# A two-layer encoder on one core: the memory heads' queries as a turned product, with 1/rms in their softmax

## The chip, the core and the metric

The kernel runs on one core of one Trainium2 chip. Its time is the device time of one execution in microseconds (us). A program measures it several times, and the kernel before has a median of 1112.88 us over three runs (1111.99 to 1113.64). TensorE (PE in the profile) multiplies and transposes, VectorE (DVE), ScalarE (ACT) and GpSimd (POOL) do the rest, and SyncE (SP) starts the transfers.

## What is computed

512 tokens of width 1024 pass through two layers. Each layer adds a token mixer with memory heads and then a gated feed-forward block (inner width 2816). The first layer's mixer is a banded attention with a sink, the second's a global one with normed queries and keys. The part that matters here is the memory heads: four heads of width 64 whose queries come from the tokens and whose keys and values come from a memory of 256 tokens.

```python
h = rms_norm(x, g_mix_pre[i])
proj = h @ w_in[i]
qm = proj[..., Q_W + 2 * KV_W:].reshape(B, S, N_MEM_HEADS, HEAD_DIM)
...
mkv = mem_n @ w_mem_kv[i]
km = mkv[..., :QM_W].reshape(B, N_MEM, N_MEM_HEADS, HEAD_DIM)
vm = mkv[..., QM_W:].reshape(B, N_MEM, N_MEM_HEADS, HEAD_DIM)
s = jnp.einsum('bshd,bmhd->bhsm', qm, km) * ATTN_SCALE
p = jax.nn.softmax(s, axis=-1)
o = jnp.einsum('bhsm,bmhd->bshd', p, vm)
```

The token heads are 12, in three groups of four with one key head each. Their outputs and the memory heads' stand side by side and go through `w_o`.

## The kernel before

Each product of fp32 numbers is made of three matmuls. A number is split into a high part (a copy rounded to the short form that TensorE takes, L286 on ScalarE or L284 on GpSimd) and a low part (the number less its high part, L290 on VectorE or L288 on GpSimd). The three products are high by high, high by low and low by high (L276, L277, L278). Weights come from memory whole, as `raw`, and are split into `whi` and `wlo`. The normed tokens are kept turned (feature on partition, token on column) as `hT`, high and low, in eight blocks of 128 features. The factor 1/rms of a token is not in `hT`; it is a column `rs` with one value for each token, and `rq` is that column times -1/8, so that queries carry the scale of the scores with a negative sign.

*Queries.* `q_pieces` (L520 to L567) makes them in chunks of four heads: c = 0, 1, 2 for the token heads, c = 3 for the memory heads. For each of four tiles of 128 tokens, eight steps of three matmuls hold a piece of `hT` as weights and let 256 columns of `whi` or `wlo` move past it, into a bank `acc` of the accumulator memory. The result, tokens on partitions, is copied out with the scale `rq` or `rs` (L538, L540, ScalarE). The token heads then get their rotary products (L440 to L443 in the first layer). The queries are split (L286, L290), four transposes (L558) of the pair [high, low] bring each head to the form feature by token, and ScalarE copies the result to `qT` (L559).

*Keys.* `keys` (L420 to L430) transposes a tile of keys twice: once as [high, low], copied by ScalarE (L426), and once as [low, high], through the bank `pv`, copied by VectorE (L430). The arrays are `ka` and `kb` for the token heads, and `kma` and `kmb` for the memory heads. A score is then two matmuls that each use all 128 rows: [q high, q low] by [k high, k low] and by [k low, k high].

*Memory heads.* `score_mem` (L600 to L620) takes two tiles of queries at a time. The scores go to a bank of the ring `s`; since the queries are negative, VectorE takes the minimum as `nm` (L614), and ScalarE computes the exponential of -1 times the score plus `nm` (L617), with the sum as `den`. Once a head's sums are there, VectorE takes the reciprocal `rd` (L630) and GpSimd multiplies p by it (L633). `turn` transposes p (L643) and splits it into `th` and `tl`; `value` multiplies it by the values (L657, L658), and a copy and an addition (L665, L666) put the result into `tok`.

*What sets the order.* Only TensorE's order is written by hand. Every piece of work is handed to `put(x, f)` with a position x in units of one head, from the table `PACE`, and the pieces run in the order of x. The tiles of queries c = 3 stood at positions from 7 + `qoff[2]` on, one `qstep` apart, among the scores, turns and values of the token heads. A scheduler orders the other engines' work. The banks limit it: two `acc`, three `s` (two once the output projection has taken the third), one `pv`, two `t`.

Of the kernel before, what the change touches and what calls it, by code (L numbers as in the profile page):

```python
# [185 lines left out]
class Trunk:  # L186
# [232 lines left out]
    def keys(self, k2, ka, kb, t, n):  # L419

        nc = self.nc
        tp = self.ps.tile([P, 4, P], F32, tag="t", name="tp", bufs=2)
        for h in range(n):
            nc.tensor.transpose(tp[:, h].bitcast(F32R), k2[:, h, :P], self.identr)
        c = slice(t * P, (t + 1) * P)
        nc.scalar.activation(ka[:, :, c], tp[:, :n], AF.Copy)  # L426
        tp = self.tagged("pv", "tp").rearrange("p (h n) -> p h n", n=P)
        for h in range(n):
            nc.tensor.transpose(tp[:, h].bitcast(F32R), k2[:, h, HD:], self.identr)
        nc.vector.tensor_copy(kb[:, :, c], tp[:, :n])  # L430


    def halves(self, x):
# [82 lines left out]
    def q_pieces(self, l, c, qTs, put, x0, lead):  # L516
# [6 lines left out]
        def prod(t, st, u):  # L523
            self.ready(t)
            if c not in qTs:
                qTs[c] = self.core.tile([P, 4, S], F32R, tag="qT", name="qT", bufs=2)
            if u == 0:
                st["ps"] = self.ps.tile([P, 512], F32, tag="acc", name="ps", bufs=2)
            ps = st["ps"]
            for k in (2 * u, 2 * u + 1):  # L530
                cs = slice((k % 4) * 256, (k % 4) * 256 + 256)
                self.mm3(ps[:, :256], self.hslice(0, k, t * P, t * P + P), self.hslice(1, k, t * P, t * P + P),
                         w[k // 4][0][:, cs], w[k // 4][1][:, cs], k == 0, k == KD - 1)
            if u == 3:
                qx = self.core.tile([P, 4, HD], F32, tag="qx", name="qx", bufs=3)
                q = ps[:, :256].rearrange("p (h d) -> p h d", d=HD)
                if l == 1 and c < 3:
                    nc.scalar.activation(qx, q, AF.Copy, scale=self.rs[:, t:t + 1])  # L538
                else:
                    nc.scalar.activation(qx, q, AF.Copy, scale=self.rq[:, t:t + 1])  # L540
                st["qx"], st["r"] = qx, None
                if c < 3:
                    st["r"] = self.rope(l, qx, t, 4, 0)

        def parts(st):
            qx, r = st["qx"], st["r"]
# [4 lines left out]

        def stage(t, st):
            if c:
                tp = self.tagged("s" if c == 3 and t > 1 else "acc", "tp").rearrange("p (h n) -> p h n", n=P)
            else:
                tp = self.ps.tile([P, 4, P], F32, tag="t", name="tp", bufs=2)
            for h in range(4):
# [7 lines left out]
                        lambda t=t, st=st: stage(t, st), lambda st=st: parts(st)))  # L565
        return out


    def score(self, hd, i):
        nc = self.nc  # L570
# [29 lines left out]
    def score_mem(self, hd, i):  # L600
# [9 lines left out]
        for z in range(2):  # L610
            qi = hd["q"]()[:, (i + z) * P:(i + z + 1) * P]
            nc.tensor.matmul(s[:, z], qi, hd["ka"](), start=True, stop=False)
            nc.tensor.matmul(s[:, z], qi, hd["kb"](), start=False, stop=True)
        nc.vector.tensor_reduce(nm[:, i:i + 2], s, axis=AX.X, op=OP.min)  # L614
        for z in range(2):
            p = self.core.tile([P, self.pbufs[0]], F32, tag="p", name="p", bufs=self.pbufs[1])
            nc.scalar.activation(p[:, :NMEM], s[:, z], AF.Exp, bias=nm[:, i + z:i + z + 1], scale=-1.0,  # L617
                                 accum_out=den[:, i + z:i + z + 1])
            hd["p"].append(p)
        if i == 2:  # L620
# [62 lines left out]
    def mixer(self, l, mkp, late, tokp):  # L683
# [68 lines left out]
        xm.append(xm[2] + pc["mdur"])  # L752
        xw = [xm[0] - pc["m0lead"], xm[1] - pc["m0lead"] + 0.01, xm[2] - pc["mlead"], xm[3] - pc["mlead"] + 0.01]
        self.mem_pieces(l, mk, put, xm, [pc["m0dur"], pc["m0dur"], pc["mdur"], pc["mdur"]], pc["mlag"], xw)
        for c in range(1, 4):
            x0 = 4 * c - 5 + pc["qoff"][c - 1]
            lay(self.q_pieces(l, c, qT, put, x0, pc["qlead"]), x0, pc["qstep"], pc["qlag"], lambda t, c=c: 4 * c + (t / 4 if c < 3 else t // 2 / 2 * pc["hstep"]))
        heads()
        xs = [max(2 * z + 1 + pc["lag"] + pc["vlag"] + 3 * pc["jstep"], 7 + 4 * pc["qstep"] + pc["qoff"][2] + pc["hoff"]) + 0.01
              for z in range(6)]  # L760
# [608 lines left out]
```

## Time and profile before

| | |
|---|---|
| median of three runs | 1112.88 us (1111.99 to 1113.64) |
| the profiled execution's own time | 1110.48 us |
| its span from first to last instruction | 1108.7 us |
| granted clock of TensorE, mean over the span | 0.999 |
| busy: TensorE, VectorE, ScalarE, GpSimd | 98%, 76%, 59%, 18% of the span |

The profile gives one execution. The mean time of an instruction is from its start to its end; on TensorE neighbours overlap, so the sum of busy times there is larger than the time that passes, and the step from one start to the next is what a matmul costs. A number in brackets at the end of a row, as in `[1.20 <-DVE kmb L430]`, is the time in which the engine had nothing to run, and the work that ended it. The memory heads' queries are computed between about 80 and 140 us in the first layer and 640 and 700 us in the second.

### The profile page before, as it was taken

Reading aid. Unit: us, or ns where it says so; the run is one execution under the profiler, and the core shown is the slowest. Engines: PE = TensorE matmul, PEld = TensorE weight load, DVE = VectorE, ACT = ScalarE, POOL = GpSimd, SP = SyncE. Lnnn points to the kernel's source line nnn. Section 1 sums busy time; section 2 is a strip of 40 time slices with the busy share of each in tenths; the row PEclk is TensorE's granted clock in tenths of the full one; section 3 lists DMA queues with packets and bytes.
Section 4 is the critical chain, followed back from the end, with each engine's and each line's share of the span. In section 5 each row is a group of like instructions: output and inputs, shape, how many; then the busy total and the mean of one; then the engine's idle time right before and its main releaser. Section 6 shows DMA issues by size and latency. Waiting matters only on the chain.

```text
span 1108.7 us, 19514 instructions
## 1 busy us (share of the span) xinstructions
PE 1089.4 (98%) x7438; PEld 1000.2 (90%) x7438; DVE 840.7 (76%) x1433; ACT 658.5 (59%) x1356; POOL 196.2 (18%) x342
## 2 busy tenths in 40 slices
PE   8999999999999999999999999999999999999997
PEld 7989978999889989998898888879999899899986
DVE  7789875999558767875788988758995478669854
ACT  6679975765445534563567888756664366346631
POOL 5683331102000000000443542212000000000001
PEclk9999999999999999999999999999999999999999
DMA  8621017343833472325543221145136123322243
GB/s 319 224 98 40 25 33 266 115 153 127 308 116 108 152 248 76 115 92 189 186 143 114 77 77 38 39 172 171 59 112 213 56 95 115 134 72 98 82 168 114
DMA packets 40558, 142.44 MB, mean 128 GB/s; under 512 B 4624, under 2 KB 5008, under 8 KB 40336
## 3 DMA queue, kind: packets, MB, share of 16 engines
q1 hardware_dynamic: 40176, 140.66, 36.8%
q8 instruction: 58, 0.95, 0.4%
q10 hardware_dynamic: 288, 0.53, 0.2%
q14 instruction: 36, 0.29, 0.1%
HBM read 122.30 MB, written 18.87 MB: 127 GB/s over the span
## 4 chain that ended last, share of the span: by engine, by line
PE 88%; DVE 5%; ACT 2%; POOL 2%; issue 1%; DMA 1%; DVEq 0%; POOLq 0%; SPq 0%; ACTq 0%
PE ps L277 14%; PE ps L276 14%; PE ps L278 14%; PE ps L1042 12%; PE ps L1041 12%; PE ps L1040 12%; PE tp L643 3%; PE o L658 2%; PE o L657 2%; PE s L582 1%; PE s L583 1%; DVE tl L290 1%; POOL r L310 1%; DVE tok L666 1%; ACT junk L314 1%
## 5 line engine op out<-in xcount | busy, mean ns | idle before, releaser
L286 ACT ACTIVATE whi<-raw 128x1024 fp32r<-128x1024 f32 (+3 forms) x205 | 168.5, 839 | 176.9 <-PE ps L1042 73.5
L290 DVE TENSOR_TENSOR wlo<-raw,whi 128x1024 fp32r<-128x1024 f32 (+3 forms) x202 | 190.9, 960 | 73.5 <-ACT whi L286 71.5
L1041 PE MATMUL ps<-sf,wlo 128*128 128x256 f32 x640 | 179.8, 281 | 0.0
L1040 PE MATMUL ps<-sf,whi 128*128 128x256 f32 x640 | 179.7, 281 | 0.0
L1042 PE MATMUL ps<-sf,whi 128*128 128x256 f32 x640 | 179.7, 281 | 0.0
L276 PE MATMUL ps<-whi,f 128*128 128x512 f32 (+1 forms) x360 | 138.7, 385 | 0.0
L277 PE MATMUL ps<-wlo,f 128*128 128x512 f32 (+1 forms) x360 | 138.5, 385 | 0.0
L278 PE MATMUL ps<-whi,f 128*128 128x512 f32 (+1 forms) x360 | 138.4, 385 | 0.0
L1042 PE MATMUL ps<-a,whi 128*128 128x256 f32 x480 | 134.4, 280 | 0.0
L1040 PE MATMUL ps<-a,whi 128*128 128x256 f32 x480 | 134.4, 280 | 0.0
L1041 PE MATMUL ps<-a,wlo 128*128 128x256 f32 x480 | 133.8, 279 | 0.0
L1041 PEld LDWEIGHTS ps<-sf,wlo 128*128 128x128 f32 x640 | 121.4, 190 | 0.5
L1040 PEld LDWEIGHTS ps<-sf,whi 128*128 128x128 f32 x640 | 121.1, 189 | 0.5
L1042 PEld LDWEIGHTS ps<-sf,whi 128*128 128x128 f32 x640 | 121.4, 190 | 0.0
L319 POOL TENSOR_SCALAR e<-sso 128x1 f32<-128x1 f32 x8 | 3.4, 420 | 563.9 <-ACT junk L314 563.7
L276 PE MATMUL ps<-whi,hT 128*128 128x256 f32 (+1 forms) x312 | 95.2, 305 | 0.0
L633 POOL TENSOR_SCALAR p<-p,rd 128x256 f32<-128x256 f32 (+2 forms) x128 | 76.5, 615 | 101.0 <-DVE rd L630 43.2
L277 PE MATMUL ps<-wlo,hT 128*128 128x256 f32 (+1 forms) x312 | 91.1, 292 | 2.9 <-DVE wlo L290 2.9
L278 PE MATMUL ps<-whi,hT 128*128 128x256 f32 (+1 forms) x312 | 90.9, 291 | 0.0
L1041 PEld LDWEIGHTS ps<-a,wlo 128*128 128x128 f32 x480 | 90.5, 188 | 0.2
L1040 PEld LDWEIGHTS ps<-a,whi 128*128 128x128 f32 x480 | 90.4, 188 | 0.2
L1042 PEld LDWEIGHTS ps<-a,whi 128*128 128x128 f32 x480 | 90.1, 188 | 0.0
(209 smaller groups left out, 2703.6 us busy)
## 6 DMA issues: line engine op xcount, KB each, us to landing
raw<-in_wgu_dram SPq DMA_DIRECT2D x48, 512.0 KB, 4.3
raw<-in_wd_dram SPq DMA_DIRECT2D x44, 512.0 KB, 4.4
rb<-in_wgu_dram SPq DMA_DIRECT2D x40, 512.0 KB, 3.6
raw<-in_wo_dram SPq DMA_DIRECT2D x17, 512.0 KB, 3.7
raw<-in_wq_dram SPq DMA_DIRECT2D x16, 512.0 KB, 5.3
xt<-x SPq DMA_DIRECT2D x12, 512.0 KB, 4.7
raw<-in_wm_dram SPq DMA_DIRECT2D x8, 512.0 KB, 4.0
x<-y SPq DMA_DIRECT2D x8, 512.0 KB, 3.0
```

The source lines that it names most:

```text
L276: mm(out, lh, rh, start=first, stop=False)
L277: mm(out, lh, rl, start=False, stop=False)
L278: mm(out, ll, rh, start=False, stop=last)
L286: a = nc.scalar.activation(hi, src, AF.Copy)
L290: b = nc.vector.tensor_sub(lo, src, hi.bitcast(F32))
L633: self.pooled = nc.gpsimd.tensor_scalar(hd["p"][z][:, :n], hd["p"][z][:, :n], rd[:, z:z + 1], 1.0, op0=OP.mult, op1=OP.mult)
L643: nc.tensor.transpose(tp[:, z], hd["p"][i][:, jj * P:(jj + 1) * P], self.ident)
L657: nc.tensor.matmul(o[:, c0:c1], hd["v"](j), th, start=(j == 0), stop=False, skip_group_check=True)
L658: nc.tensor.matmul(o[:, c0:c1], hd["v"](j), tl, start=False, stop=last, skip_group_check=True)
L1040: mm(out, wh[:, s], rh, start=start and k == 0, stop=False, skip_group_check=True)
L1041: mm(out, wl[:, s], rh, start=False, stop=False, skip_group_check=True)
L1042: mm(out, wh[:, s], rl, start=False, stop=k == 3, skip_group_check=True)
```

## The change

Three things are altered.

1. The memory heads' queries leave `q_pieces`. A new function `memory_queries` makes them turned from the start: for each of two halves z (two heads, 128 columns of the weight), the columns of `whi` and `wlo` are held as weights and all 512 tokens of `hT` move past them, eight steps of three matmuls into one bank `acc`. Feature is on partition and token on column, so no transpose follows. ScalarE copies the two heads' high parts to `qT`, 64 rows by 512 columns each, and VectorE writes the two low parts, 64 by 512 each, into the other 64 rows. For the second head of a half the high part stands in the lower rows of `qT` and the low part in the upper, so its halves are the other way round; since both orders of the keys are used in the sum, the score is the same.
2. 1/rms of a token varies along the columns there, so the queries stay without it. The scores of a pair of tiles have tokens on partitions, and the factor comes in there: VectorE takes the maximum `mx`, multiplies it by `rq` to give `nm`, and the exponential takes its scale from the column `rp` = -`rq`, which GpSimd makes once a layer.
3. In `keys`, the memory keys' second copy (four heads) goes to ScalarE; the token keys' stays with VectorE.

The eight steps of each half stand a quarter of `qstep` apart, from the same first position as before, so that both halves together take the span that the four tiles took.

```diff
@@ keys
-        nc.vector.tensor_copy(kb[:, :, c], tp[:, :n])
+        if n == NMH:
+            nc.scalar.activation(kb[:, :, c], tp[:, :n], AF.Copy)
+        else:
+            nc.vector.tensor_copy(kb[:, :, c], tp[:, :n])
@@ q_pieces: stage
-                tp = self.tagged("s" if c == 3 and t > 1 else "acc", "tp").rearrange("p (h n) -> p h n", n=P)
+                tp = self.tagged("acc", "tp").rearrange("p (h n) -> p h n", n=P)
@@ new
+    def memory_queries(self, l, qTs, put, x0, lead, step):
+
+        nc = self.nc
+        w, ps = {}, {}
+        for z in range(2):
+            self.unit(self.a["wq"][l, 3, z], self.side(l, "qw", 6 + z), put=put, x=x0 - lead + z * lead / 3, dst=w,
+                      key=z, pair=("wq", l, 3, z))
+
+        def prod(z, k):
+            if k == 0:
+                ps[z] = self.tagged("acc")
+            c = slice((k % 4) * 256 + P * z, (k % 4) * 256 + P * z + P)
+            wh, wl = [x[:, c] for x in w[k // 4]]
+            self.mm3(ps[z], wh, wl, self.hslice(0, k, 0, S), self.hslice(1, k, 0, S), k == 0, k == KD - 1)
+            if k < KD - 1:
+                return
+            if z == 0:
+                qTs[3] = self.core.tile([P, 4, S], F32R, tag="qT", name="qT", bufs=2)
+                self.rp = self.small.tile([P, NT], F32, tag="rp", name="rp", bufs=2)
+                nc.gpsimd.tensor_scalar(self.rp, self.rq, -1.0, 1.0, op0=OP.mult, op1=OP.mult)
+            rows = (slice(0, HD), slice(HD, P))
+            q = [qTs[3][:, 2 * z + h] for h in range(2)]
+            for h in range(2):
+                nc.scalar.activation(q[h][rows[h]], ps[z][rows[h]], AF.Copy)
+            for h in range(2):
+                nc.vector.tensor_sub(q[h][rows[1 - h]], ps[z][rows[h]], q[h][rows[h]].bitcast(F32))
+
+        for z in range(2):
+            for k in range(KD):
+                put(x0 + (2 * z + k / 4) * step, lambda z=z, k=k: prod(z, k))
@@ score_mem
-        nc.vector.tensor_reduce(nm[:, i:i + 2], s, axis=AX.X, op=OP.min)
+        mx = self.small.tile([P, 2], F32, tag="mx", name="mx", bufs=3)
+        nc.vector.tensor_reduce(mx, s, axis=AX.X, op=OP.max)
+        nc.vector.tensor_mul(nm[:, i:i + 2], mx, self.rq[:, i:i + 2])
...
-            nc.scalar.activation(p[:, :NMEM], s[:, z], AF.Exp, bias=nm[:, i + z:i + z + 1], scale=-1.0,
+            nc.scalar.activation(p[:, :NMEM], s[:, z], AF.Exp, bias=nm[:, i + z:i + z + 1],
+                                 scale=self.rp[:, i + z:i + z + 1],
                                  accum_out=den[:, i + z:i + z + 1])
@@ the mixer's list of pieces
-        for c in range(1, 4):
+        for c in range(1, 3):
             x0 = 4 * c - 5 + pc["qoff"][c - 1]
-            lay(self.q_pieces(l, c, qT, put, x0, pc["qlead"]), x0, pc["qstep"], pc["qlag"], lambda t, c=c: 4 * c + (t / 4 if c < 3 else t // 2 / 2 * pc["hstep"]))
+            lay(self.q_pieces(l, c, qT, put, x0, pc["qlead"]), x0, pc["qstep"], pc["qlag"], lambda t, c=c: 4 * c + t / 4)
+        self.memory_queries(l, qT, put, 7 + pc["qoff"][2], pc["qlead"], pc["qstep"])
```

Three places show what it does to the order. The first is TensorE in the first layer, where the third tile's product, or now the second half's, begins. Here `ps` is the bank of the queries, `tp` a transpose, `p` the softmax of a token head, `th` and `tl` its split transpose, and `o` a head's output. A row names the output, then the moving operand and the weights. Before:

```order
L276 MATMUL ps_1917<-whi_1582,hT_115 128x256
L277 MATMUL ps_1917<-wlo_1583,hT_115 128x256
L278 MATMUL ps_1917<-whi_1582,hT_117 128x256
L643 MATMUL tp_1924<-cst_87,p_1718 128x128
L643 MATMUL tp_1924<-cst_87,p_1742 128x128
L643 MATMUL tp_1924<-cst_87,p_1763 128x128
L558 MATMUL tp_1932<-identr_91,q2_1834 128x128 x4
L657 MATMUL o_1938<-th_1869,vs_246 128x256
L658 MATMUL o_1938<-tl_1870,vs_246 128x256
```

and after:

```order
L276 MATMUL ps_1891<-hT_115,whi_1582 128x512
L277 MATMUL ps_1891<-hT_117,whi_1582 128x512
L278 MATMUL ps_1891<-hT_115,wlo_1583 128x512
L678 MATMUL tp_1895<-cst_87,p_1714 128x128
L678 MATMUL tp_1895<-cst_87,p_1735 128x128
L678 MATMUL tp_1895<-cst_87,p_1753 128x128
L692 MATMUL o_1903<-th_1841,vs_246 128x256
L693 MATMUL o_1903<-tl_1842,vs_246 128x256
```

Each group of three narrow products with `hT` as weights (two of them stand there before, one is shown) has become one of three wide products with the weight matrix as weights, and the group L558 behind the turn is gone.

The second place is VectorE at the end of the second half, where `tok` is written for a token head, `nm` is the maximum of a tile and `q2` a tile of queries before its transpose. Before:

```order
L666 TENSOR_TENSOR tok_888<-o_2051,tmp_2130 64x512
L629 TENSOR_TENSOR den_2023<-den_2023,es_2114 128x4
L588 ISA p_2154,nm_2149<-s_2151,mask_210,nsink_89 128x256
L588 ISA nm_2149 128x1
L630 RECIPROCAL rd_2113<-den_2023 128x4
L290 TENSOR_TENSOR tl_2146<-tp_2141,th_2145 128x384
L290 TENSOR_TENSOR tl_2168<-tp_2163,th_2167 128x384
L588 ISA p_2183,nm_2149<-s_2180,mask_210,nsink_89 128x384
L588 ISA nm_2149 128x1
L290 TENSOR_TENSOR q2_2186<-qx_2139,q2_2186 128x4x64
```

and after:

```order
L701 TENSOR_TENSOR tok_888<-o_1992,tmp_2062 64x512
L664 TENSOR_TENSOR den_1974<-den_1974,es_2046 128x4
L620 ISA p_2085,nm_2080<-s_2082,mask_210,nsink_89 128x256
L620 ISA nm_2080 128x1
L665 RECIPROCAL rd_2045<-den_1974 128x4
L595 TENSOR_TENSOR qT_1868<-ps_1891,qT_1868 64x512 x2
L290 TENSOR_TENSOR tl_2077<-tp_2072,th_2076 128x384
L290 TENSOR_TENSOR tl_2099<-tp_2094,th_2098 128x384
L620 ISA p_2108,nm_2080<-s_2105,mask_210,nsink_89 128x384
L620 ISA nm_2080 128x1
```

The two subtractions of the second half stand ahead of the two `tl`; the last tile's split, which stood behind them, is gone.

The third place is VectorE in the first layer while the memory keys are made. There `rt` and `qx` belong to the rotary products of a tile of queries, and `den`, `es` and `rd` to the first token head. Before:

```order
L430 CAST kmb_816<-tp_929 128x4x128
L588 ISA p_938,nm_879<-s_935,mask_210,nsink_89 128x256
L588 ISA nm_879 128x1
L440 TENSOR_TENSOR rt_958<-qx_956,cst_87 128x64
L442 TENSOR_TENSOR qx_956<-qx_956,cst_87 128x4x16
L430 CAST kmb_816<-tp_968 128x4x128
L629 TENSOR_TENSOR den_880<-den_880,es_942 128x4
L443 TENSOR_TENSOR qx_956<-qx_956,rt_958 128x4x16
L630 RECIPROCAL rd_941<-den_880 128x4
```

and after:

```order
L620 ISA p_938,nm_879<-s_935,mask_210,nsink_89 128x256
L620 ISA nm_879 128x1
L664 TENSOR_TENSOR den_880<-den_880,es_942 128x4
L665 RECIPROCAL rd_941<-den_880 128x4
L620 ISA p_979,nm_974<-s_976,mask_210,nsink_89 128x256
L620 ISA nm_974 128x1
L443 TENSOR_TENSOR rt_958<-qx_956,cst_87 128x64
L445 TENSOR_TENSOR qx_956<-qx_956,cst_87 128x4x16
L446 TENSOR_TENSOR qx_956<-qx_956,rt_958 128x4x16
```

Both copies L430 are gone from VectorE, `den` and `rd` have moved up to right behind the last maximum, and the three rotary products stand behind the next head's first maximum.

More of the change, by code (lines that the diff above doesn't have):

```diff
@@ L536, in prod @@
                 q = ps[:, :256].rearrange("p (h d) -> p h d", d=HD)
-                if l == 1 and c < 3:
+                if l:
                     nc.scalar.activation(qx, q, AF.Copy, scale=self.rs[:, t:t + 1])
@@ L540, in prod @@
                     nc.scalar.activation(qx, q, AF.Copy, scale=self.rq[:, t:t + 1])
-                st["qx"], st["r"] = qx, None
-                if c < 3:
-                    st["r"] = self.rope(l, qx, t, 4, 0)
+                st["qx"], st["r"] = qx, self.rope(l, qx, t, 4, 0)
         def parts(st):
```

## The prediction, made before the changed kernel ran

> **What bounds the kernel now.** I read the totals first, then the chain that ended last, then the windows of the stage that the change touches, and last the timeline around each wait in it.
>
> ```profile
> PE 1089.4 (98%) x7438; PEld 1000.2 (90%) x7438; DVE 840.7 (76%) x1433; ACT 658.5 (59%) x1356; POOL 196.2 (18%) x342
> PE 88%; DVE 5%; ACT 2%; POOL 2%; issue 1%; DMA 1%; DVEq 0%; POOLq 0%; SPq 0%; ACTq 0%
> ```
>
> TensorE is busy 98% of the span and holds 88% of the chain: a TensorE instruction that goes is worth its step, as long as nothing else is late just behind it. That has to be asked of each stretch, so the windows come next (window: length, then busy us of PE, PEld, DVE, ACT, POOL).
>
> ```profile
> 80.00:110.00 30.00, 29.46 (x233) 28.36 (x234) 26.94 (x87) 27.13 (x79) 11.42 (x19) 1.00 0.12 36
> 110.00:126.00 16.00, 16.00 (x134) 15.93 (x133) 12.88 (x41) 14.13 (x43) 4.70 (x9) 1.00 0.11 34
> 126.00:147.00 21.00, 19.26 (x130) 16.97 (x129) 19.80 (x49) 20.36 (x58) 8.00 (x16) 1.00 0.17 51
> 640.00:680.00 40.00, 39.69 (x275) 35.19 (x273) 32.79 (x61) 32.45 (x76) 15.90 (x22) 1.00 0.15 54
> 680.00:700.00 20.00, 19.36 (x123) 16.48 (x122) 18.17 (x32) 18.89 (x45) 6.91 (x11) 1.00 0.15 54
> ```
>
> Up to 126 us in layer 0 and 680 us in layer 1 TensorE is full and the others have a tenth or more to spare. In the stretch behind that, where the last token heads and the first memory heads overlap, VectorE and ScalarE are nearly full (19.80 and 20.36 of 21.00) and TensorE is the one with gaps. The memory queries are worked on in both kinds of stretch.
>
> **The products.** Per layer 96 matmuls with 256 columns become 48 with 512. Busy means overlap, so the price is the step from start to start.
>
> ```profile
> 110.90 0.28 PE L276 MATMUL ps<-whi,hT 128*128 128x256 f32 x1
> ...
> 111.61 0.49 PE L643 MATMUL tp<-cst,p 128*128 128x128 f32 x3
> ```
> ```profile
> 53.41 0.40 PE L276 MATMUL ps<-whi,mT 128*128 128x512 f32 x1
> ...
> 54.11 0.39 PE L276 MATMUL ps<-whi,mT 128*128 128x512 f32 x1
> ```
>
> Six narrow ones (two weight rows of three products) take 111.61 - 110.90 = 0.71 us, 0.118 each; three wide ones 0.70 us, 0.233 each. So 96 x 0.118 = 11.4 us become 48 x 0.233 = 11.2 us: -0.2 a layer, **-0.3** for both after rounding. Halving the count of matmuls is worth next to nothing, since the columns streamed stay the same.
>
> **The transposes** (L558, four of 128x128 for each of four token tiles, both layers) go altogether, with what feeds them: per tile a copy from the accumulator, a split on ScalarE and VectorE, and the copy back.
>
> ```profile
> 118.52 0.54 PE L558 MATMUL tp<-identr,q 128*128 128x128 f32 x4
> 118.89 0.35 PE L657 MATMUL o<-th,vs 128*128 128x256 f32 x1
> ```
>
> From the group's start to the next product is 0.37 us; eight groups make **-3.0**. The matmul behind a group starts its successor late, but in the order a group of L643 stands just ahead and keeps that. Three of the eight (the third and fourth tile's of layer 0, the third's of layer 1) stand in front of a wait for someone else:
>
> ```profile
> 131.13 0.54 PE L558 MATMUL tp<-identr,q 128*128 128x128 f32 x4
> 132.19 0.39 PE L657 MATMUL o<-th,vs 128*128 128x256 f32 x1 [0.52 <-DVE tok L666]
> ...
> 133.73 0.41 PE L643 MATMUL tp<-cst,p 128*128 128x128 f32 x2 [0.68 <-DVE tl L290]
> ...
> 139.63 0.39 PE L657 MATMUL o<-th,vs 128*128 128x256 f32 x1 [0.23 <-DVE tok L666]
> ```
> ```profile
> 689.24 0.63 PE L643 MATMUL tp<-cst,p 128*128 128x128 f32 x4 [0.64 <-DVE tl L290]
> ```
>
> There VectorE is late anyway, and TensorE would only wait longer. I take back the smaller of 0.37 and the wait behind it: 0.37 + 0.23 + 0.37 = **+1.0**. If the relief below shortens these waits, nothing is taken back; the four waits together (0.52 + 0.68 + 0.23 + 0.64 = 2.1) are also what that relief could give at most.
>
> **What ScalarE and VectorE do instead.** The nearest rows:
>
> ```profile
> 131.25 0.47 ACT L540 ACTIVATE qx<-ps,rq 128x256 f32<-128x256 f32 x1
> L286 ACT ACTIVATE q<-qx 128x256 fp32r<-128x256 f32 x32 | 13.3, 416 | 17.3 <-DVE qx L443 7.9 <-DVE qx L548 7.7 <-DVE rd L630 1.5
> L559 ACT ACTIVATE qT<-tp 128x512 fp32r<-128x512 f32 x32 | 19.1, 597 | 0.8 <-PE tp L558 0.5
> L665 ACT ACTIVATE tmp<-o 64x512 f32<-64x512 f32 x32 | 18.9, 592 | 9.4 <-PE o L658 8.9
> L290 DVE TENSOR_TENSOR q<-qx,q 128x256 fp32r<-128x256 f32 x32 | 15.5, 485 | 5.5 <-ACT q L286 5.1
> L666 DVE TENSOR_TENSOR tok<-o,tmp 64x512 f32<-64x512 f32 x32 | 22.0, 686 | 7.8 <-ACT tmp L665 7.5
> 139.68 0.16 DVE L629 TENSOR_TENSOR den<-den,es 128x4 f32<-128x4 f32 x1
> 140.00 0.47 ACT L617 ACTIVATE p<-s,nm 128x256 f32<-128x256 f32 x1
> 143.31 0.28 PE L612 MATMUL s<-kma,qT 128*128 128x256 f32 x1
> ```
>
> ScalarE loses 4 x (0.47 + 0.42 + 0.60) = 6.0 us a layer and gets four copies of 64x512 (the row of L665) for 2.4 us, and two key copies of 0.6. VectorE loses four splits, 1.9 us, and the two key copies; it gets four subtractions of 64x512 (the row of L666), 2.7 us, and eight products of 128x2 for nm, at 0.16 each 1.3 us. So ScalarE gains 2.4 us a layer, and VectorE works about 0.9 us more.
>
> What matters is where it lies. The list of VectorE in the section on the change shows both subtractions of the second half in one piece, 1.2 us at the pitch of such rows, ahead of the two tl that the wait at 133.73 was for; before, one split of 0.6 stood behind them. Ahead of the piece one split is gone and one of the tok splits is further forward, 0.5 and 0.6. That puts the piece at no cost up to 1.2 us of longer wait per layer; the row nearest to it is that 0.68 wait, which shows the spot has no slack, but most of the piece is paid for ahead of it. I take a quarter, **+0.6** for two layers. The products of nm stand between the maximum and the exponential of a pair. The banks of scores bound them from zero to 16 x 0.16 = 2.6; I take zero, since a score pair's bank is used again only two pairs later: the pair written at 143.31 takes the bank whose exponentials ended at 140.00 + 0.47 = 140.5, with 2.8 us between. The new product rp on GpSimd (128x4) has 1/rms long before it is needed and stands among idle time. The scale of the exponential comes from a column instead of a constant: L540 has such a column and costs its 0.47 as L617 does without, so nothing. No transfer changes in size or count; SyncE's order differs in one swapped pair of weight halves, which stand in the same lead time.
>
> **The keys' second copy** (layer 0, L429 to L430) has a wait of its own.
>
> ```profile
> 60.80 0.45 PE L424 MATMUL tp<-identr,k 128*128 128x128 f32 x4
> 62.45 0.51 PE L429 MATMUL tp<-identr,k 128*128 128x128 f32 x4 [1.20 <-DVE kmb L430]
> ...
> 66.15 0.33 PE L643 MATMUL tp<-cst,p 128*128 128x128 f32 x1 [0.40 <-POOL p L633]
> 66.87 0.33 PE L643 MATMUL tp<-cst,p 128*128 128x128 f32 x1 [0.39 <-POOL p L633]
> ```
> ```profile
> 61.62 0.68 DVE L430 CAST kmb<-tp 128x512 fp32r<-128x512 f32 x1
> ```
> ```profile
> 61.52 0.58 ACT L426 ACTIVATE kma<-tp 128x512 fp32r<-128x512 f32 x1
> 62.00 0.47 ACT L540 ACTIVATE qx<-ps,rq 128x256 f32<-128x256 f32 x1
> ...
> 63.24 0.28 ACT L628 ACTIVATE es<-nm,sink 128x4 f32<-128x4 f32 x1
> ```
> ```profile
> 61.93 2.53 POOL L288 TENSOR_TENSOR wlo<-raw,whi 128x512 fp32r<-128x512 f32 x2
> 65.61 2.22 POOL L633 TENSOR_SCALAR p<-p,rd 128x256 f32<-128x256 f32 x4 [1.15 <-DVE rd L630]
> ```
>
> The wait of 1.20 does not go. ScalarE's copy would begin behind kma at 62.00 and end at 62.6, later than VectorE's 62.30: +0.3. The gain is further on. VectorE, rid of the copy, reaches den and rd of head 0 some 1.5 us sooner (rd ends at 65.4 now; es, ScalarE's part, is ready at 63.24 + 0.28 = 63.5), and GpSimd, free at 61.93 + 2.53 = 64.5, starts the normalising of p there and not at 65.61. The two waits for p, with the late steps that they cause 1.2 us, then go. Net **-0.9**; between -1.2 and +0.3. In layer 1 TensorE does not wait for that copy: zero.
>
> Rows of two engines bear on this:
>
> ```profile
> 63.33 1.22 DVE L442 TENSOR_TENSOR qx<-qx,cst 128x64 f32<-128x64 f32 x1
> 70.95 0.22 DVE L443 TENSOR_TENSOR qx<-qx,rt 128x64 f32<-128x64 f32 x1
> ```
> ```profile
> 70.56 2.24 POOL L633 TENSOR_SCALAR p<-p,rd 128x256 f32<-128x256 f32 x4 [2.73 <-DVE qx L442]
> ```
>
> The rotary product took 1.22 us beside GpSimd's L288, and the rotary sum of another tile 0.22 beside GpSimd's normalising, which ran from 70.56 on. In the new order these products move beside that normalising. If they are held there too, head 1's scores come 1.22 - 0.22 = 1.0 us later and the keys' term is near zero; by the row at 70.95 they are not, so the sum keeps -0.9. The Trainium skill, "SBUF — State Buffer", section "Who interferes with whom", says that a VectorE instruction with two SBUF inputs contends with any GpSimd instruction that reads SBUF. By that rule the keys' term would be zero and the sum -1.7; the row at 70.95 does not agree with it.
>
> **Sum.** -0.3 - 3.0 + 1.0 + 0.6 - 0.9 = -2.6 us. The profiled execution took 1110.48 us (span 1108.7); it would become 1107.9. The median of the three runs is 2.4 us above that execution, so 1112.88 - 2.6 = **1110.3 us**. A measurement of this kernel tells about 0.2%, 2.2 us, from no change, so this lies just on the far side of it.
>
> **Rivals.**
> - *Swallowed.* VectorE and ScalarE set the pace from 126 and from 680 us on; all that TensorE saves there and the lead it brings becomes a longer wait. For it: 19.80 and 20.36 of 21.00 busy. Against: ScalarE gains 2.4 us a layer, and five of the eight transposes lie where TensorE is full. Left over are about -1.2: 1111.7 us.
> - *Relieved.* The lighter ScalarE sets the late tok and tl free: the +1.0 and the +0.6 fall away, and of the 2.1 us of waits most go: -4.2 to -6.0, about 1107.8 us.
> - *Rotary products held* beside the normalising near 65 us: the keys' 0.9 is gone, -1.7, 1111.2 us. For it: the 1.22 of 63.33; against: the 0.22 of 70.95. This is the case that the page on the state buffer would make.
> - *Slower: the pieces at the ends of the two halves.* At four places (two halves, two layers) 1.0 us of copies on ScalarE and then 1.2 us of subtractions on VectorE stand in one piece in front of th, tl and tok. From the point where th or tok has less slack than that, TensorE waits; with all four exposed in full 8.8 - 4.2 + 1.0 = +5.6: 1118.5 us. For it: the wait at 133.73, where the slack is below zero. Against: the first halves end near 117 and 670 us, where VectorE has a fifth to spare.
> - *That it does not do what it says* is ruled out: the order has 48 wide products and no memory transposes.
>
> **How the numbers follow.** Forecast (-2.2 to -4.2) 0.34, relieved 0.18, swallowed 0.30, held 0.06, slower 0.12. Faster by over 0.2%: 0.34 + 0.18 = 0.52; within: 0.30 + 0.06 = 0.36; slower: 0.12. The range goes from -6.0 (relieved) to +2.1, which leaves out most of the slower case and the end of the relieved one: 1106.9 to 1115.0.
>
> **What would show it.** Right: the last q transposes of layer 0 at about 112 us, those of the token heads; the wide products at 0.233; the waits for POOL near 66 us gone while the one at L429 stays; the wait for tl behind the second half not longer than 1 us. Wrong: TensorE idle at 130 to 147 us grown by more than 1.5 us (swallowed), waits for th, tl or tok right behind the four pieces of over 1 us each (slower), or a new wait of TensorE for a bank of scores in the memory heads, which would make the zero for nm wrong.

## The result: slower by about one per cent

| | before | changed |
|---|---|---|
| median, same chip | 1112.43 us (1110.63 to 1113.64, 4 runs) | 1123.86 us (1123.47 to 1125.79, 4 runs) |
| ratio to before | | 1.011, 95% interval 1.0098 to 1.0122 |
| profiled execution, its span | 1110.48, 1108.7 us | 1125.79, 1124.0 us |

The prediction said 1110.3 us, with a range up to 1115.0. The page of the changed kernel, its totals and its chain by engine:

```profile
PE 1097.7 (98%) x7310; PEld 1001.8 (89%) x7310; DVE 843.8 (75%) x1445; ACT 660.2 (59%) x1344; POOL 199.2 (18%) x344
PE 82%; DVE 9%; ACT 4%; POOL 2%; issue 1%; DMA 1%; DVEq 0%; POOLq 0%; ACTq 0%; SPq 0%
```

TensorE has 128 matmuls less and is busy 8 us more, so many matmuls have become longer. VectorE's and ScalarE's shares of the chain have about doubled, from 5% and 2%, so TensorE waits for them more. These are two different losses. The waits first (total, times, longest), of the kernel before and of the changed one:

```profile
PE tp L643 <- DVE tl L290: 2.5, 7, 0.7
...
PE tp L429 <- DVE kmb L430: 1.2, 1, 1.2
```
```profile
PE tp L678 <- DVE tl L290: 7.5, 8, 2.4
PE tp L429 <- ACT kmb L431: 2.8, 2, 1.5
```

The waits for `tl` have tripled, and those for the second copy of the memory keys have more than doubled. The longest wait for `tl` stands behind the second half of the queries. The timeline there, of TensorE, ScalarE and VectorE:

```profile
138.22 0.34 PE L615 MATMUL s<-kb,qT 128*128 128x384 f32 x1
140.94 0.50 PE L678 MATMUL tp<-cst,p 128*128 128x128 f32 x2 [2.38 <-DVE tl L290]
141.10 0.65 PE L692 MATMUL o<-th,vs 128*128 128x384 f32 x1
...
141.88 0.63 PE L276 MATMUL ps<-whi,th 128*128 128x512 f32 x1
142.30 0.63 PE L277 MATMUL ps<-wlo,th 128*128 128x512 f32 x1
```
```profile
137.59 1.20 ACT L593 ACTIVATE qT<-ps 64x512 fp32r<-64x512 f32 x2
138.80 0.49 ACT L286 ACTIVATE th<-tp 128x384 fp32r<-128x384 f32 x1
```
```profile
138.81 1.39 DVE L595 TENSOR_TENSOR qT<-ps,qT 64x512 fp32r<-64x512 f32 x2 [0.52 <-ACT qT L593]
140.24 1.02 DVE L290 TENSOR_TENSOR tl<-tp,th 128x384 fp32r<-128x384 f32 x2
```

It is a staircase. ScalarE's two copies take 1.20 us and hold up `th`; VectorE's two subtractions wait for both copies, then take 1.39 us and hold up `tl`; TensorE waits for `tl`. Two more of the four ends of a half have such a wait:

```profile
123.95 0.56 PE L678 MATMUL tp<-cst,p 128*128 128x128 f32 x2 [2.09 <-DVE tl L290]
...
698.89 0.63 PE L678 MATMUL tp<-cst,p 128*128 128x128 f32 x4 [1.86 <-DVE tl L290]
```

The first half's end in layer 0 looks the same. At the second half's end in layer 1 VectorE does not sit idle ahead of the subtractions, but they stand ahead of `tl` all the same. The first half's end in layer 1 has no such wait.

Behind the wait the wide product takes 0.63 us and not 0.40, and its step is 0.42 (142.30 - 141.88). The windows around the two waits of layer 0 tell why (length, busy us of PE, PEld, DVE, ACT, POOL, granted clock as a share of the full one, DMA):

```profile
120.66:124.07 3.41, 1.32 (x10) 0.94 (x9) 2.85 (x9) 2.48 (x6) 2.06 (x4) 1.00 0.00 0
124.07:127.48 3.41, 3.41 (x11) 3.12 (x11) 1.41 (x5) 0.98 (x3) 0.00 (x0) 0.50 0.00 0
137.72:141.13 3.41, 1.03 (x7) 0.74 (x7) 2.85 (x8) 3.37 (x9) 2.06 (x4) 1.00 0.53 154
141.13:144.54 3.41, 3.41 (x12) 3.02 (x11) 2.00 (x6) 1.46 (x5) 0.00 (x0) 0.50 0.02 5
```

TensorE's granted clock is 0.50 for the 3.41 us behind each. Two such stretches cost some 1.7 us each. (The profiled execution has a third one at 14.84 us, which would account for most of the 1.9 us by which it is above the median.) The kernel before has none until the last microseconds of the span.

The second loss is far from the change, in the feed-forward block of the second layer, which it does not touch. The window from 1005 to 1045 us, of the kernel before and of the changed one, with matmuls of 256 columns only:

```profile
1005.00:1045.00 40.00, 40.00 (x345) 40.00 (x345) 35.91 (x54) 24.51 (x42) 0.00 (x0) 1.00 0.30 104
```
```profile
1005.00:1045.00 40.00, 40.00 (x336) 40.00 (x335) 34.87 (x53) 23.51 (x41) 0.00 (x0) 1.00 0.32 106
```

Both run without a gap at full clock, yet one starts 345 matmuls in 40 us and the other 336: 0.116 and 0.119 us each. The same instruction lags by 10.2 us at 783 us and by 15.0 us at 1050.

### The profile page after: what moved, and what is told of

Same layout as the page of the kernel before. It is cut to its first block, busy times and chain, and to the rows that moved or that the text cites. A ratio compares the mean times of both kernels' runs of the same rounds, so it can differ in the third digit from the quotient of the medians.

```text
span 1124.0 us, 19273 instructions
## 1 busy us (share of the span) xinstructions
PE 1097.7 (98%) x7310; PEld 1001.8 (89%) x7310; DVE 843.8 (75%) x1445; ACT 660.2 (59%) x1344; POOL 199.2 (18%) x344
## 4 chain that ended last, share of the span: by engine, by line
PE 82%; DVE 9%; ACT 4%; POOL 2%; issue 1%; DMA 1%; DVEq 0%; POOLq 0%; ACTq 0%; SPq 0%
PE ps L277 13%; PE ps L278 13%; PE ps L276 13%; PE ps L1078 12%; PE ps L1077 12%; PE ps L1076 12%; PE tp L678 2%; PE o L693 2%; PE o L692 1%; DVE tl L290 1%; PE s L614 1%; PE s L615 1%; ACT p L626 1%; DVE tok L701 1%; DVE nm L625 1%
## 5 line engine op out<-in xcount | busy, mean ns | idle before, releaser
L278 PEld LDWEIGHTS ps<-whi,f 128*128 128x128 f32 x360 | 67.6, 188 | 13.5
L276 PEld LDWEIGHTS ps<-whi,f 128*128 128x128 f32 x360 | 67.7, 188 | 13.0
L277 PEld LDWEIGHTS ps<-wlo,f 128*128 128x128 f32 x360 | 67.7, 188 | 12.8
```

The source lines that it names most:

```text
L276: mm(out, lh, rh, start=first, stop=False)
L277: mm(out, lh, rl, start=False, stop=False)
L278: mm(out, ll, rh, start=False, stop=last)
```

## The experiments

Three theories were set against each other. A: the pieces at the ends of the halves, with the halved clock behind them. B: the keys' copy on ScalarE. C: something in the wide products or the softmax. Behind the first four runs came D: where the operands lie in memory. The ratio is to the kernel before on the same chip.

### The keys' copy put back

```diff
-        if n == NMH:
-            nc.scalar.activation(kb[:, :, c], tp[:, :n], AF.Copy)
-        else:
-            nc.vector.tensor_copy(kb[:, :, c], tp[:, :n])
+        nc.vector.tensor_copy(kb[:, :, c], tp[:, :n])
```

> The changed kernel with the memory keys' second copy on VectorE again. Theory A (the copies on ScalarE and the subtractions on VectorE at the ends of the halves hold the split transposes back, TensorE is idle for over 2 us and its clock is then halved for 3.4 us): the waits for the halves and the two stretches of half clock stay, the wait for the keys' copy in layer 1 (1.3 us in the changed kernel) goes, the waits for p near 66 us come back (0.8): 1122.5 to 1124. Rival B (the keys' copy on ScalarE is what costs): below 1116.

Measured: 1122.78 us, 1.0108 (1.0094 to 1.0122). The wait in layer 1, which the changed kernel had there, went:

```profile
PE tp L429 <- ACT kmb L431: 1.3, 1, 1.3
```

The waits for p came back, and the half clocks stayed. B falls as the main cause.

### The keys' copy alone

The same edit in the other direction, in the kernel before.

> The kernel before with only the memory keys' second copy moved to ScalarE. A: between -0.9 (layer 0, as the prediction had it) and +1.6 us (the new wait of 1.3 in layer 1 and 0.3 in layer 0): 1111.5 to 1114. Rival B: 1119 or more.

Measured: 1113.37 us, 1.0020 (1.0009 to 1.0030), so a small loss. Its waits for the copy (two, total 3.2, the longest 1.7), and GpSimd and VectorE beside each other in layer 0:

```profile
PE tp L429 <- ACT kmb L431: 3.2, 2, 1.7
```
```profile
61.83 2.52 POOL L288 TENSOR_TENSOR wlo<-raw,whi 128x512 fp32r<-128x512 f32 x2
64.76 2.08 POOL L636 TENSOR_SCALAR p<-p,rd 128x256 f32<-128x256 f32 x4 [0.41 <-DVE rd L633]
```
```profile
63.19 1.18 DVE L632 TENSOR_TENSOR den<-den,es 128x4 f32<-128x4 f32 x1 [1.19 <-ACT es L631]
...
65.34 0.54 DVE L445 TENSOR_TENSOR qx<-qx,cst 128x64 f32<-128x64 f32 x1
```

GpSimd's normalising starts at 64.76 and not at 65.61, as worked out, and the waits for p are gone: the matmul that stood at 66.87 stands at 65.87. But `den`, an addition of four columns, takes 1.18 us until L288 ends (64.37 and 64.35), and the rotary products take 0.43 to 0.54 beside the normalising. They end at 65.31, 65.88 and 66.45, each 0.07 behind the end of one of GpSimd's four normalising instructions (65.24, 65.82, 66.38), so each was held until the instruction then at work was done. By 80 us the lead is gone (the same instruction is 0.1 us late), and in layer 1 the copy brings a wait of its own.

### The pieces apart

```diff
-            for h in range(2):
-                nc.scalar.activation(q[h][rows[h]], ps[z][rows[h]], AF.Copy)
-            for h in range(2):
-                nc.vector.tensor_sub(q[h][rows[1 - h]], ps[z][rows[h]], q[h][rows[h]].bitcast(F32))
+            def evict(h):
+                nc.scalar.activation(q[h][rows[h]], ps[z][rows[h]], AF.Copy)
+                nc.vector.tensor_sub(q[h][rows[1 - h]], ps[z][rows[h]], q[h][rows[h]].bitcast(F32))
+
+            for h in range(2):
+                put(x0 + (2 * z + 1.75) * step + (0.3, 0.8)[h], lambda h=h: evict(h))
```

> The changed kernel with the copy and the subtraction of each head put 0.3 and 0.8 of a head's time behind the end of the half, apart from each other. A: TensorE's waits of 2.1, 2.4 and 1.9 us for tl fall below 0.7 each, no stretch of half clock in layer 0 is left, and 4.5 us of waits and 3.4 us of slow clock go: 1113 to 1116. Rival C (the wide products themselves, or the scale in the softmax, make the kernel slower): 1122 to 1124.

Measured: 1119.86 us, 1.0076 (1.0063 to 1.0089), above what was expected. The waits of this kernel:

```profile
PE ps L276 <- DVE qT L595: 3.4, 2, 1.9
...
PE tp L681 <- DVE tl L290: 2.4, 9, 0.5
```

A was right on `tl`: 2.4 us in all and none above 0.5, as before the change. Two new waits came, for the bank that the output projection needs (0.8 of a head's time was too late behind the second half), and the lag in the feed-forward block stayed. A stretch of half clock is left in layer 0, where A expected none: it starts at 64.57, behind a wait of 2.56 for the keys' copy.

### Head by head, at the same place

```diff
             for h in range(2):
                 nc.scalar.activation(q[h][rows[h]], ps[z][rows[h]], AF.Copy)
-            for h in range(2):
                 nc.vector.tensor_sub(q[h][rows[1 - h]], ps[z][rows[h]], q[h][rows[h]].bitcast(F32))
```

> The changed kernel with copy, subtraction, copy, subtraction written in this order, head by head, at the same place. A: only one copy and one subtraction stand ahead of tl, so each wait at the end of a half is about 1.2 us shorter, below 1.3 us, and no clock is halved: 1115 to 1119, between the spread kernel and the changed one. Rival C: 1123 to 1124.

Measured: 1119.42 us, 1.0074 (1.0061 to 1.0088). That is 0.4 us above what A expected, and level with the kernel that has the pieces apart, not behind it. The order of two lines is worth 0.4%: the scheduler then lets a subtraction start behind the first copy and `tl` pass ahead of the second. One wait of 1.92 was left, at the second half's end in layer 0, with one stretch of half clock behind it; A expected none above 1.3 and no half clock.

### The layout alone

```diff
             nc.gpsimd.memset(self.mhalf, -0.5)
+            nc.gpsimd.memset(self.small.tile([P, 8], F32, tag="pad", name="pad", bufs=1), 0.0)
```

> The kernel before, with 32 more bytes in the pool of small tiles and nothing else (one tile that nobody reads, set to zero once). That moves the base addresses of whi, wlo and all that lies behind them by 32, as the tiles mx and rp of the change do (by 160, which is 32 modulo 64). Theory D (part of the loss is where the operands lie: with moving operand and weights alike modulo 64 bytes a 256-column matmul takes 119.2 ns, with them 32 apart 117.1): in the second layer's feed-forward block the step goes from 117 to 119-120 ns and the time up by 4 to 6 us, to 1115 to 1118. Rival (the slower step comes from the new order or from the clock): 1110.5 to 1112.5, no change.

Measured: 1118.18 us, 1.0064 (1.0049 to 1.0079). A tile that nobody reads costs 7 us:

```profile
1005.00:1045.00 40.00, 40.00 (x336) 40.00 (x335) 34.87 (x52) 23.79 (x40) 0.00 (x0) 1.00 0.31 106
```

No piece of the change is in this kernel, and its loss comes only in the feed-forward blocks (it is 0.1 us behind at 200 us, 0.7 at 230, 2.3 at 700, 2.8 at 802, and 7.8 at the end).

### The layout back, modulo 64

The same line in the changed kernel.

> The changed kernel with 32 bytes more in the same pool, so that whi and wlo lie as in the kernel before. D: 4 to 6 us faster than the changed kernel, 1118 to 1120, with the two stretches of half clock in layer 0 still there and steps of 117 in the second layer's feed-forward block. Rival: 1123 to 1125.

Measured: 1126.29 us, 1.0140 (1.0123 to 1.0157): a miss. Its window shows 335 matmuls in the 40 us. So it is not the place modulo 64. Of the stretches of half clock that were expected, the one behind the second half is there (138.99); the other stands at 63.90, behind a wait of 2.54 for the keys' copy.

### The pieces apart, the copy back, 32 bytes

```diff
-                put(x0 + (2 * z + 1.75) * step + (0.3, 0.8)[h], lambda h=h: evict(h))
+                put(x0 + (2 * z + 1.75) * step + ((0.3, 0.8), (0.1, 0.4))[z][h], lambda h=h: evict(h))
```

> The changed kernel with the 32 bytes, the keys' second copy on VectorE again, and each head's copy and subtraction apart: 0.3 and 0.8 of a head's time behind the first half, 0.1 and 0.4 behind the second, so that the bank is free before the output projection asks for it. If layout, pieces and key copy are all that the change lost: 1107 to 1111, about where the prediction stood. If something else in it costs (the products, the scale in the softmax): 1113 or more.

Measured: 1119.37 us, 1.0075 (1.0060 to 1.0090). No stretch of half clock is left until the end of the span. At the end of the first mixer it is level with the kernel before (0.2 us ahead at 162 us) and at the last matmul 7.9 us behind, most of it from the feed-forward blocks, with 335 matmuls in the window.

### The softmax part alone

The kernel before with queries copied without scale, `mx`, the product by `rq` and the scale `rp`, and 32 bytes.

> The kernel before with only the 1/rms of the memory heads moved into the softmax (queries copied without scale, maximum, product by rq, scale of the exponential from a column) and the layout kept. The prediction put nothing on it, with bounds of 0 and 2.6 us: 1111 to 1113.6. Theory A and D need it below 1 us; the rival that it lies in the path of the scores: 1113 to 1114.

Measured: 1120.11 us, 1.0082 (1.0067 to 1.0097), above both expectations. The layout was not kept: with `mx`, `rp` and the 32 bytes all behind them moves by 192 bytes, as in the kernel of "The layout back, modulo 64". Of the 10.4 us by which the profile is behind at the last matmul, 8.7 come in the feed-forward blocks. In the first layer's mixer there is one new wait, shown with VectorE's rows ahead of it:

```profile
143.15 0.39 PE L617 MATMUL s<-kma,qT 128*128 128x256 f32 x1 [1.70 <-ACT p L624]
```
```profile
140.36 0.68 DVE L620 TENSOR_REDUCE mx<-s 128x2 f32<-128x512 f32 x1
...
141.04 0.53 DVE L290 TENSOR_TENSOR tl<-tp,th 128x384 fp32r<-128x384 f32 x1
141.49 0.32 DVE L621 TENSOR_TENSOR nm<-mx,rq 128x2 f32<-128x2 f32 x1
```

The maximum is ready at 141.0, but the small product stands behind a `tl` and starts at 141.5; the exponential comes later still, and the scores wait for its bank. Other waits get shorter: between 123 and 150 us the lag grows by 0.2 us only (1.0 to 1.2). In the changed kernel and the mended ones no wait for a bank of scores appears.

### The layout back, modulo 256

The tiles `mx` and `rp` had moved all that lies behind them by 160 bytes; 96 more make 256.

```diff
-            nc.gpsimd.memset(self.small.tile([P, 8], F32, tag="pad", name="pad", bufs=1), 0.0)
+            nc.gpsimd.memset(self.small.tile([P, 24], F32, tag="pad", name="pad", bufs=1), 0.0)
```

> The changed kernel with 96 more bytes in the pool of small tiles, so that whi and wlo lie where they lay before modulo 256 bytes (32 bytes more had brought them back only modulo 64, and the step stayed at 119 to 122 ns). Theory D2 (the step of a 256-column matmul depends on the distance of its two operands modulo 256 bytes: 116.7 ns at 32, 119 to 120 at 0, 96 and 128): steps of 116.7 in the second layer's feed-forward block and 5 to 7 us less than the changed kernel: 1116.5 to 1119. Rival (any change of the program slows these steps, wherever the operands lie): 1122 to 1126.

Measured: 1117.48 us, 1.0060 (1.0046 to 1.0074), as D2 expected:

```profile
1005.00:1045.00 40.00, 40.00 (x345) 40.00 (x344) 35.66 (x53) 24.63 (x42) 0.00 (x0) 1.00 0.34 113
```

The waits and stretches of half clock in layer 0 are still there. So 96 bytes that nobody reads take back half of the loss. This kernel and the one with 32 bytes more differ in nothing but the width of that tile, so the slower step comes neither from the tile's instruction nor from the new order.

### All mended, modulo 256

> The changed kernel with the pieces apart, the keys' copy on VectorE and whi and wlo back modulo 256. D2, with pieces and key copy as measured: the 7.5 us by which the same kernel with 32 bytes falls behind in the feed-forward blocks go, 1110.5 to 1113, within 0.2% of the kernel before. Rival: 1118 to 1120.

Measured: 1112.15 us, 1.0011 (1.0001 to 1.0020). The whole loss but 0.1% is found. The profile shows where a part of the rest can lie. It is 0.3 us behind the kernel before at 60 us, 2.7 at 66, and 1.8 at the last matmul; between the first two stands the wait for the memory keys, which is 1.20 us in the kernel before:

```profile
64.24 0.67 PE L429 MATMUL tp<-identr,k 128*128 128x128 f32 x4 [2.68 <-DVE kmb L430]
```

A stretch of half clock follows. Such a wait, of 2.5 to 2.7 us with half clock behind it, stands in four of the 16 profiles, and one of the four is a kernel without any piece of the change ("Distance or place", below), so it does not need the change. How often it comes in the executions without a profile is not known.

### The mended kernel, first layer shifted too

```diff
             self.hp = self.pool(hs[0], "hT0")
+            nc.gpsimd.memset(self.hp.tile([P, 8], F32, tag="pad", name="padh", bufs=1), 0.0)
@@
         pools["f"] = self.pool(ff, f"f{l}")
+        if l == 0:
+            self.nc.gpsimd.memset(pools["f"].tile([P, 56], F32, tag="pad", name="padf", bufs=1), 0.0)
```

> The same, with 32 bytes ahead of the first layer's hT, so that there too the operands of the feed-forward block's output product lie 32 apart (they lay 0 apart, 119.6 ns), and the hidden tiles kept where they were. D2: 960 matmuls by 2.9 ns and some of the 864 beside them by 2 ns, 3 to 5 us less than the mended kernel: 1106 to 1109.5.

Measured: 1108.75 us, 0.9978 (0.9968 to 0.9987): the fastest kernel of the study, and faster than the one before.

### The kernel before, shifted

The same edit in the kernel before.

> The kernel before with the same 32 bytes ahead of the first layer's hT and nothing of the change. D2: 3 to 5 us less than before, 1106 to 1109. It also shows whether the mended change is worth anything beside it: the prediction's -2.6 would put the mended one ahead by that, no gain would put both level.

Measured: 1109.98 us, 0.9987 (0.9978 to 0.9997), 1 us above what was expected. The profiled execution took 1107.01 us, 3.5 less than that of the kernel before; the others took up to 1112.56. The interval overlaps with that of the mended kernel, so the change itself isn't shown to be worth anything once its losses are mended. The two profiled executions have the same layout, which makes them a pair. The same instructions in the shifted kernel before, and in the mended one:

```profile
6.23 0.44 PE L486 MATMUL ps<-whi,hT 128*128 128x384 f32 x1
...
133.35 0.30 PE L643 MATMUL tp<-cst,p 128*128 128x128 f32 x1 [0.68 <-DVE tl L290]
135.50 0.48 PE L276 MATMUL ps<-whi,th 128*128 128x512 f32 x1
...
685.80 0.30 PE L643 MATMUL tp<-cst,p 128*128 128x128 f32 x1 [0.64 <-DVE tl L290]
694.95 0.33 PE L643 MATMUL tp<-cst,p 128*128 128x128 f32 x1
```
```profile
6.77 0.60 PE L486 MATMUL ps<-whi,hT 128*128 128x384 f32 x1
...
132.58 0.33 PE L678 MATMUL tp<-cst,p 128*128 128x128 f32 x1 [0.16 <-DVE tl L290]
135.63 0.50 PE L276 MATMUL ps<-whi,th 128*128 128x512 f32 x1 [0.59 <-DVE qT L592]
...
684.55 0.33 PE L678 MATMUL tp<-cst,p 128*128 128x128 f32 x1 [0.15 <-DVE tl L290]
695.11 0.33 PE L678 MATMUL tp<-cst,p 128*128 128x128 f32 x1 [0.59 <-DVE tl L290]
```

The mended kernel starts 0.54 us late, is 0.77 ahead at 133 us, and 0.13 behind at 135.6. In layer 1 it is 1.25 ahead at 685 and 0.16 behind at 695. So the mended kernel gains 1.3 us in the first layer. Of this 0.5 is the shorter wait for `tl` (0.16 and not 0.68), and 0.8 was there ahead of it. At the end of the second half 0.9 of the 1.3 is lost again, and in layer 1 all that was gained.

### Distance or place

The shifted kernel before, with 64 bytes more in the pool of small tiles: the operands of the product with the gate and up weights in the first layer's feed-forward block lie 32 apart, but at another place. (This is the product that the expectations call the output product.)

> The kernel before with 32 bytes ahead of the first layer's hT and 64 more in the pool of small tiles: the operands of the first layer's output product lie 32 apart modulo 256, but at 32 and 0 and not at 224 and 192; those of the second layer's lie 224 apart, at 224 and 0. Distance decides: 116.7 ns a step in the first layer for the products from hT, another value in the second. Place decides: 119 ns or more in the first layer too.

Measured: 1112.80 us, one run. The step is 116.7 ns in the first layer and 118.3 in the second, so between distance and place it is distance that decides. The mean step from start to start of 256-column matmuls with `whi` or `wlo` as weights, from the traces, by the base addresses of both operands modulo 256:

| moving operand | weights | distance | step, ns | in |
|---|---|---|---|---|
| 224 | 192 | 32 | 116.7 | before, layer 1 |
| 32 | 0 | 32 | 116.7 | this kernel, layer 0 |
| 224 | 0 | 224 | 118.3 | this kernel, layer 1 |
| 192 | 192 | 0 | 119.6 | before, layer 0 |
| 96 | 96 | 0 | 119.2 | the changed kernel, layer 0 |
| 128 | 128 | 0 | 119.5 | changed, modulo 64, layer 0 |
| 224 | 224 | 0 | 120.0 | 32 bytes alone, layer 1 |
| 224 | 96 | 128 | 119.6 | the changed kernel, layer 1 |
| 224 | 128 | 96 | 120.0 | changed, modulo 64, layer 1 |

Each row is the mean over 960 matmuls of one profile, those of the feed-forward block whose moving operand is `sf` (sums of blocks of the turned tokens). The addresses are those that the compiled program gives its tiles. Two things in the traces do not fit the distance alone. At distance 0 the place shows too, with 119.2 to 120.0. And the 912 matmuls beside them, whose moving operand is one of those blocks itself (`a`), have both operands at the same addresses (224 and 192) in the first layer of the kernel before and of the shifted one, and yet take 117.9 ns in one and 116.9 in the other.

### The second half's pieces earlier

```diff
-((0.3, 0.8), (0.1, 0.4))[z][h]
+((0.3, 0.8), (0.05, 0.2))[z][h]
```

> The mended and shifted kernel with the pieces behind the second half at 0.05 and 0.2 of a head's time and not at 0.1 and 0.4. If the bank that the output projection waits for (0.6 us behind the last subtraction, first layer) is what takes the transposes' gain back there: that wait goes, 0.6 us or less beyond the spread of the runs, 1107.5 to 1108.5. If VectorE is simply full there: the wait appears in front of tl, 1108.5 to 1109.

Measured: 1110.34 us, 0.9984 (0.9975 to 0.9994): above both expectations, and not better. The waits for `tok`, of the mended and shifted kernel (with its wait for the bank) and of this one:

```profile
PE o L692 <- DVE tok L701: 2.5, 6, 0.7
...
PE ps L276 <- DVE qT L592: 0.6, 1, 0.6
```
```profile
PE o L692 <- DVE tok L701: 2.8, 5, 0.9
...
PE tp L678 <- DVE nm L648: 0.5, 1, 0.5
```

The wait for the bank is gone. Instead there is a new wait for `nm` and 0.3 us more for `tok`; the waits for `tl`, where the second expectation looked for it, are 2.4 us and not 3.1. From 130 to 137 us of the mended and shifted kernel VectorE is busy for 6.45 us of 7.00 and ScalarE for 6.88, so there is little room on either. Which of the two holds TensorE back was not tested.

## Why the prediction was wrong

In ratios to before, the loss of 1.1% splits into 0.5% for the layout (changed 1.0110, layout back 1.0060), 0.5% for the pieces with their clock and the keys' copy (1.0060 to 1.0011), and 0.1% that is left.

- **The layout was not in the sum at all.** The tiles `mx` and `rp` were looked at for what they compute and not for the 160 bytes by which they move `whi` and `wlo`. This step is missing: "No transfer changes in size or count" was the only thing asked about memory. No row of the kernel before said that it matters, but its two layers ran the same product at 119.6 and 116.7 ns, and that difference was there to be asked about.
- **The pieces were mis-sized.** The prediction put a quarter of 1.2 us a layer on them, "most of the piece is paid for ahead of it". What it named for payment (a split that goes, a `tok` split further forward) stands ahead of the piece on VectorE's queue, but the subtractions did not start before ScalarE's two copies had ended, and at both ends in layer 0 VectorE sat idle for 0.52 us just there. The waits came to 2.09, 2.38 and 1.86 us, at three of the four ends. The rival "slower" had the right mechanism, and its price of 1.0 + 1.2 us at each of the places was about the measured one at these three; it got a chance of 0.12 because the windows gave VectorE a fifth to spare near 117 us. A mean over 16 us says nothing of a queue that is served in order: the first half's wait of 2.09 came in just such a stretch.
- **The clock** was not in any of the cases: each long wait in layer 0 cost 1.7 us more.
- **Products and transposes** were right as far as the traces show. Three wide products take 0.70 us. The two terms make 1.65 us a layer; in the trace of the mended kernel the lead grows by 1.3 us in the first layer and 1.2 in the second, and 0.5 of each is a shorter wait for `tl`.
- **"I take back the smaller of 0.37 and the wait behind it"** took back too little. With the pieces mended, 0.9 of the 1.3 us in the first layer and all of the lead in the second is gone at the end of the second half. In that kernel "swallowed" is what came, and its reason fits: VectorE and ScalarE have little room there.
- **The product of nm** at zero holds in the changed kernel, where no wait for a bank of scores appears; alone in the old order it made a wait of 1.70, within the bounds of 0 and 2.6, most of which came back in shorter waits.
- **The keys' copy** failed in both layers. In layer 0 the 0.9 us came (1.0) and was lost within 13 us. The rotary products were held, each until the end of a normalising instruction, and so for 0.43 to 0.54 us; 0.22 and 1.22 had been weighed. The row at 70.95 was misread as evidence against that: the product ran from 70.95 to 71.17, over the end of the first normalising instruction (70.56 to 71.04), so it had next to nothing to wait for. In layer 1 "TensorE does not wait for that copy: zero" was right for VectorE and wrong for ScalarE: 1.30 us.

What stays open: why the step depends on the distance of the operands, what else sets it in the products of `a`, and how much of the 5.4 us for pieces and keys' copy in the mended kernel belongs to each, since the keys' copy cost 0.2% alone and 0.02% (within the interval) beside the rest.

## What to carry to other kernels

When a change adds or removes tiles, even a few bytes, compare the base addresses of the operands of the heaviest matmuls before and after, and look at the step of a loop that the change does not touch. An instruction pair on two in-order queues (copy on one engine, subtraction on the next) is priced as a staircase with what stands behind it on each queue, not by mean busy shares; written head by head, or put at a later place, it lets the urgent work pass. Before a time is put down to a change, run the same layout without the change.

## What the runs showed of the hardware

- **The granted clock goes by windows.** Inside the span the half clock always lasts 3.41 us, on a grid of that length. In the 16 profiles 14 such stretches followed a grid window in which TensorE was busy for 0.21 to 0.49 of the time, and one followed 0.52; 14 windows between 0.52 and 0.59 were followed by none, and one with 0.46 wasn't either. So a wait of 1.9 us cost 1.7 more or nothing, by where it lay on the grid: 1.92 in the head-by-head kernel did, 1.86 at 698.89 did not. The Trainium skill, "TensorE: Matmul & The Clock Gate", section "Part 1: The HAM clock gate", gives the same free-running window and a halved clock after an idle one. The traces agree with the window of 3.41 us; but a window that was busy for somewhat less than half was enough. In the softmax kernel a window of 0.52 kept the clock:

```profile
141.50:144.91 3.41, 1.76 (x11) 1.58 (x12) 3.15 (x7) 2.64 (x8) 3.23 (x4) 1.00 0.19 30
144.91:148.32 3.41, 3.41 (x26) 3.06 (x25) 3.00 (x8) 2.94 (x8) 0.45 (x1) 1.00 0.34 129
```

- **A matmul's step depends on the distance of its two operands in memory** modulo 256 bytes: with 256 columns and `sf` as moving operand 116.7 ns at 32 and 118.3 to 120.0 at the other distances seen (0, 96, 128, 224), with the engine never idle and the clock at 1.00. The products of `a` show that it is not the only thing that counts (117.9 and 116.9 at the same two addresses).
- **A small VectorE instruction can wait for GpSimd**: an addition of 128x4 took 1.18 us until GpSimd's subtraction ended, and 0.16 elsewhere. Rotary products of 128x64 took 0.43 to 0.54 us beside the normalising, each until 0.07 us behind the end of one of its instructions, and 0.21 with GpSimd idle (65.14 in the kernel before).
